# One decoder layer on one core: x transposed without its row factor, the factor applied after the products, fresh tiles for the first weights, and all low parts on VectorE

## The chip, the cores and the metric

The program runs on one core of a Trainium2 chip. The core has TensorE (PE, matmuls and transposes), VectorE (DVE), ScalarE (ACT), GpSimd (POOL) and SyncE (SP), which here only issues transfers. The metric is the device time of one execution in microseconds (us); lower is better.

## The reference, cut to what matters

One trunk layer on 256 tokens of width 1024:

```python
a = rms_norm(h, mix_norm_g[i])
z = a @ w_in[i]                       # 1024 x 3584, columns: q_a k_a v_a q_h f_h i_h g_h, 512 each
q = partial_rope(rms_norm(q, q_norm_g[i]), positions) * (ATTN_HEAD_DIM ** -0.5)
k = partial_rope(rms_norm(k, k_norm_g[i]), positions)
attn = dilated_attention(q, k, v).reshape(B, S, ATTN_WIDTH)
rec = hgrn2_mixer(q_h, f_h, i_h, g_h, lower_bounds[i], hgrn_norm_g[i])
h = h + jnp.concatenate([attn, rec], axis=-1) @ w_out[i]
m = rms_norm(h, ffn_norm_g[i])
h = h + moe_ffn(m, router_w[i], ...)  # 32 experts, top 4, every expert's 12 MB of f32 weights are read
h = h + (p[i] @ ple_proj[i]) * jax.nn.sigmoid(h @ ple_gate[i])
```

`rms_norm` multiplies each row (token) by one number, its row factor 1/sqrt(mean(x^2) + eps), and each column by g.

## The kernel before, in words

**Stages.** (1) The front: x is loaded and normalised, the seven z chunks of 512 columns are multiplied in the order ka, fh, qa, qh, va, ih, gh, and the attention and HGRN work on finished chunks is woven between the matmuls of the later chunks; then comes the product with w_out ("wo"). (2) Router and gates. (3) The 32 experts, each four gate-up tiles and two down tiles of 2 MB. (4) The last gate with `ple_gate` and the output.

**Products in two parts.** z and wo need more than one rounded pass: each f32 operand is split into a high part (rounded to fp32r) and a low part (the rest), and three matmuls are added: high x high, high x low, low x high. Weights are split in `split`: of every 1 MB tile ("place" 0 to 17: two per z chunk, four for wo) ScalarE writes two high parts (L249) and DVE or GpSimd subtracts two low parts (L250); the list `POOL_FIRST` names the places whose subtracts go to GpSimd, 10 of the 18. The parts live in a ring of 12 buffers (`highs`), three places' worth, so the split of place n waits until PE has used place n - 3.

**x.** `row_rstd` squares x (one half on ScalarE L307, one on DVE L308) and takes the power -0.5 on GpSimd (L302). A diagonal matrix `dg` of the row factors is built (L375), 16 matmuls x^T @ dg transpose and scale x (L380), and each of the eight 128-column blocks leaves PSUM times g as high part `ahi` (ScalarE L385) and low part `alo` (DVE L386).

**Order.** The order on each engine is set by a scheduler when the program is built. The list `STEPS` says after which half chunk which steps of the attention stream (q and k norms `qk_norm`, rotation, scores) and of the HGRN stream (`hgrn_f`, `hgrn_q`, the eight levels of `hgrn_levels`) come. The names used below: L653/L656/L302/L663/L664 are square, sum, power, scale by row, scale by g of a q or k norm; L675 to L680 the rotation, L687 the transposes behind it; L544, L546/L547, L556/L557, L583, L587 are one HGRN level (difference, two exponentials, two products, matmuls, masked copy).

**Memory.** Weights and large intermediates share a pool of 2 MB tiles (`Memory`), each of two halves; a 1 MB request takes a free half of a tile that is open, the first found. `fill` issues the next weight loads on SP's queue as tiles come free; the first 10 expert tiles are loaded while the front runs, and from then on each load waits for a tile to be used up.

Of the kernel before, what the change touches and what calls it, by code (L numbers as in the profile page):

```python
# [23 lines left out]
EPS = 1e-6  # L24
# [60 lines left out]
class Memory:  # L85
# [3 lines left out]
    def __init__(self):  # L89
        self.pools, self.room, self.tiles = [], [], []  # L90

# [4 lines left out]
    def open(self, kind):  # L96

        for k, n in enumerate(self.room):
            if n:
                self.room[k] -= 1  # L100
                g = dict(pool=k, kind=kind, busy=[0, 0], t=self.pools[k].tile([128, 4096], kind, name="g", tag="g"))
# [14 lines left out]

    def take(self, n, kind, shape):
        g = n == 1 and self.half(kind) or self.open(kind)
        assert g, ("full", n, kind)
        i = g["busy"].index(0) if n == 1 else 0  # L120
        g["busy"][i:i + n] = [1] * n
        a = g["t"][0:shape[0], 2048 * i:2048 * i + int(np.prod(shape[1:]))]
        if len(shape) > 2:
            names = "abc"[:len(shape) - 1]
            a = a.rearrange("p (%s) -> p %s" % (" ".join(names), " ".join(names)), **dict(zip(names[1:], shape[2:])))
        return a, (g, i, n)

# [9 lines left out]
def layer(ctx, tc, A, at):  # L137
# [60 lines left out]
    place = {k: i for i, k in enumerate(seq)}  # L198
    st = {"next": 0, "raw": 0, "cap": 0, "split": 0, "keep": 0}
    raw, parts, owner = {}, {}, {}  # L200
# [4 lines left out]
    def fill():  # L205
        while st["raw"] < st["cap"] and st["next"] < len(seq):
            k = seq[st["next"]]
            n = 2 if big(k) else 1
            keep = max([st["keep"]] + [a - len(held) for a in TILES[len(log):]])
            if not M.can(n) or M.left() - n < keep:  # L210
# [9 lines left out]
            else:  # L220
                shape = [128, 4, 512]
            t, i = M.take(n, F32, shape)
            if not place[k] or k == (("D", E - 1), 1):
# [59 lines left out]

    for tt in range(2):
        sp.dma_start(h[:, tt, :], A["x"][0, tt * 128:(tt + 1) * 128, :])
    ident = const("ident")
    rows = pers.tile([24, 128], F32, name="rows")
    sp.dma_start(rows[0:8], A["mix_norm_g"].rearrange("o (j p) -> (o j) p", p=128))
# [4 lines left out]
    gcol = pers.tile([128, 32], F32, name="gcol")  # L293

    power = pers.tile([128, 16], F32, name="power")
    pool.memset(power, -0.5)
# [32 lines left out]

    rstd = row_rstd("x")  # L330
    ahi = S.new([128, 8, T], F32R, "ahi")
# [32 lines left out]

    p0 = bank()
    pe.transpose(p0[:, :24], rows, ident[:24, :24])
    for k in range(2):
        pe.transpose(p0[:, 24 + 4 * k:28 + 4 * k], rows2[:, k:k + 255:2], ident[:4, :4])
    act.activation(gcol[:, 0:24], p0[:, :24], AF.Copy)
    act.activation(gcol[:, 24:32].rearrange("p (j k) -> p k j", k=2), p0[:, 24:32].rearrange("p (k j) -> p k j", k=2), AF.Copy)  # L370


    dg = carve(256).rearrange("p (a d) -> p a d", a=2)
    for tt in range(2):
        dve.tensor_scalar(dg[:, tt, :], ident, rstd[:, tt:tt + 1], None, op0=OP.mult)  # L375
    for j in range(0, 8, 2):
        b = bank()
        for jj in range(2):
            for tt in range(2):
                pe.matmul(b[:, jj * 256 + tt * 128:jj * 256 + tt * 128 + 128], h[:, tt, (j + jj) * 128:(j + jj) * 128 + 128],  # L380
                          dg[:, tt, :], start=True, stop=True)
        for jj in range(2):
            s = b[:, jj * 256:jj * 256 + 256]
            g = gcol[:, j + jj:j + jj + 1]
            act.activation(ahi[:, j + jj, :], s, AF.Copy, scale=g)  # L385
            dve.scalar_tensor_tensor(alo[:, j + jj, :], s, g, ahi[:, j + jj, :].bitcast(F32), op0=OP.mult, op1=OP.subtract)  # L386

# [101 lines left out]
    def hgrn_f(p):  # L489
# [4 lines left out]
        s, lf = B["W"]  # L494
        act.activation(s, p, AF.Sigmoid)
        yield
# [94 lines left out]
    def hgrn_gate(p):  # L591
        G2 = S.new([128, 2, 1024], F32, "G2")
        B.update(gt=G2[:, 0], oo=G2[:, 1])
        act.activation(B["gt"], p, AF.Tanh, scale=0.5)
        yield
# [5 lines left out]
    def hgrn_out():  # L601
# [48 lines left out]
    def qk_norm(p, gi, dst, scale):  # L650
# [125 lines left out]
    def evac(n):  # L776
        def f(p):
            act.activation(lazy(n), p, AF.Copy)
            yield
        return f  # L780
# [63 lines left out]
    def squares(n):  # L844
        for tt in range(2):
# [4 lines left out]
            else:  # L850
                act.activation(o, hs_, AF.Square, accum_out=ss4[:, n, tt:tt + 1])

    def busy(t, n, i):

        for k in range(n):
            with tc.issue_after(i):
                i = pe.matmul(t[:, 0:128], ones, ones, start=True, stop=True).ins

# [434 lines left out]
```

## Time and profile before

| | |
|---|---|
| median of 3 runs | 1148.01 us (1146.41 to 1151.06) |
| profiled execution | 1148.54 us, span 1146.8 us |
| PE busy | 1062.8 us (93% of the span) |
| DVE busy | 324.2 us (28%) |
| ACT busy | 204.8 us (18%) |
| POOL busy | 80.4 us (7%) |
| read from HBM | 430.51 MB, 376 GB/s over the span |

The span is the time from the first to the last event of the profiled execution, and the execution's own time is 1.7 us more. Busy shares are means over four stages with different limits, so the rows further down are cut by stage.

### The profile page before, as it was taken

How to read it: one execution, taken by the hardware profiler on the slowest of the kernel's cores; microseconds unless marked ns; L12 is line 12 of the kernel's file. 1: busy time of each engine (PE TensorE's matmuls, PEld its weight loads, DVE VectorE, ACT ScalarE, POOL GpSimd, SP SyncE). 2: the span in 40 equal slices, each digit the busy share in tenths (PEclk: the TensorE clock that was granted, in tenths of full speed). 3: DMA queues.
4: the chain of work that ended last, by engine and by line, in shares of the span. 5: the costliest groups of instructions: out<-in, count | busy, mean ns of one | idle time of the engine just before them, and what ended most of it. 6: DMA issues, size and time to landing. Idle time of an engine off the chain costs nothing. (4 is left out here: it accounts for less than half of the span.)

```text
span 1146.8 us, 12108 instructions
## 1 busy us (share of the span) xinstructions
PE 1062.8 (93%) x5045; PEld 467.3 (41%) x5045; DVE 324.2 (28%) x627; ACT 204.8 (18%) x395; POOL 80.4 (7%) x76
## 2 busy tenths in 40 slices
PE   6899899999999999999999999899999999999877
PEld 5787674333333333333333333333333333333235
DVE  5878733222121111211111111111211121111143
ACT  5646531011111111111111111111101111110030
POOL 4651140000000000000000000000000000000000
PEclk9999899999999999999999999999999999999998
DMA  8842568999999999999999999999989999999961
GB/s 287 288 149 87 203 264 366 427 428 426 427 429 427 428 428 428 427 428 427 427 427 429 428 428 426 414 426 427 427 348 419 427 424 428 429 427 427 429 253 37
DMA packets 44692, 432.41 MB, mean 377 GB/s; under 512 B 5980, under 2 KB 7672, under 8 KB 19928
## 3 DMA queue, kind: packets, MB, share of 16 engines
q1 hardware_dynamic: 44232, 430.66, 90.1%
q0 software_dynamic: 400, 0.92, 0.2%
q8 instruction: 42, 0.69, 0.2%
q14 instruction: 18, 0.15, 0.0%
HBM read 430.51 MB, written 1.05 MB: 376 GB/s over the span
## 5 line engine op out<-in xcount | busy, mean ns | idle before, releaser
L1108 PE MATMUL bk<-g,x 128*64 128x512 f32 x2048 | 468.8, 596 | 4.2 <-DMA g<-in_expert_w_gate_up 4.2
L1108 PEld LDWEIGHTS bk<-g,x 128*64 128x64 f32 x2048 | 144.9, 137 | 282.0 <-issue 263.5
L1142 PE MATMUL bk<-g,ht 128*64 128x512 f32 x1024 | 235.1, 596 | 16.3 <-DMA g<-in_expert_w_down 16.3
L1142 PEld LDWEIGHTS bk<-g,ht 128*64 128x64 f32 x1024 | 73.4, 137 | 154.2 <-issue 144.0
L1120 ACT ACTIVATE sgm<-gm 128x512 f32<-128x512 f32 x32 | 20.2, 630 | 377.4 <-DVE gm L1119 377.4
L1119 DVE TENSOR_SCALAR gm<-bk 128x512 f32<-128x512 f32 x32 | 22.1, 692 | 206.3 <-PE bk L1108 204.8
L925 PE MATMUL bk<-h,sx 128*64 128x512 f32 x256 | 67.0, 610 | 0.0
L1082 DVE TENSOR_SCALAR sg<-c_slot,posx,gates 128x128 f32<-128x128 f32 x64 | 19.3, 344 | 166.9 <-PE bk L1085 166.9
L917 POOL CAST sb<-c_sel 128x128 fp32r<-128x128 f32 x32 | 9.4, 296 | 810.2 <-PE bk L1098 802.8
L940 DVE TENSOR_TENSOR x<-bk,gcol 128x256 f32<-128x256 f32 x64 | 24.2, 420 | 131.8 <-PE bk L936 131.8
L1149 DVE SCALAR_TENSOR_TENSOR ylo<-bk,gs,yhi 128x512 fp32r<-128x512 f32 x32 | 24.0, 750 | 122.4 <-ACT yhi L1148 116.2
L250 POOL TENSOR_TENSOR lo<-g,hi 128x1024 fp32r<-128x1024 f32 x20 | 54.5, 2744 | 53.7 <-ACT hi L249 40.2
L1157 PE MATMUL pz<-yhi,so 64*128 64x512 f32 x128 | 29.3, 445 | 21.5 <-ACT yhi L1148 17.9
L1148 ACT ACTIVATE yhi<-bk,gs 128x512 fp32r<-128x512 f32 x32 | 22.0, 687 | 139.9 <-PE bk L1142 139.9
L249 ACT ACTIVATE hi<-g 128x1024 fp32r<-128x1024 f32 x36 | 37.4, 1056 | 19.8 <-issue 7.8
L1132 ACT ACTIVATE ht<-bk 128x512 f32<-128x512 f32 x32 | 19.1, 598 | 116.6 <-PE bk L1130 116.6
L927 ACT ACTIVATE xr<-bk 128x512 f32<-128x512 f32 x32 | 19.1, 597 | 112.1 <-PE bk L925 112.1
L914 DVE TENSOR_SCALAR sx<-c_slot,posx,rstd 128x64 f32<-128x64 f32 x64 | 17.2, 312 | 62.2 <-PE bk L925 62.2
L1157 PE MATMUL pz<-ylo,so 64*128 64x512 f32 x128 | 28.9, 440 | 5.4 <-DVE ylo L1149 5.4
L435 PE MATMUL pz<-hi,g 128*128 128x512 f32 x80 | 32.4, 405 | 1.6 <-DVE g L663 0.8
L437 PE MATMUL pz<-hi,g 128*128 128x512 f32 x80 | 32.2, 403 | 0.0
L436 PE MATMUL pz<-lo,g 128*128 128x512 f32 x80 | 31.9, 399 | 0.0
(254 smaller groups left out, 928.3 us busy)
## 6 DMA issues: line engine op xcount, KB each, us to landing
g<-in_expert_w_gate_up SPq DMA_DIRECT2D x128, 2048.0 KB, 31.9
g<-in_expert_w_down SPq DMA_DIRECT2D x63, 2048.0 KB, 36.1
g<-in_w_in SPq DMA_DIRECT2D x13, 1024.0 KB, 5.7
g<-in_w_out SPq DMA_DIRECT2D x4, 1024.0 KB
g<-in_ple_gate SPq DMA_DIRECT2D x4, 1024.0 KB, 18.6
g<-in_expert_w_down SPq DMA_DIRECT2D x2, 1024.0 KB, 35.5
h<-in_x SPq DMA_DIRECT2D x2, 512.0 KB, 4.3
g<-in_w_in SPq DMA_DIRECT2D x2, 512.0 KB, 4.4
```

The lines of the kernel that those rows point to most:

```text
L249: act.activation(hi, w[:, o:o + 2], AF.Copy)
L250: (pool if i in POOL_FIRST else dve).tensor_tensor(lo, w[:, o:o + 2], hi.bitcast(F32), OP.subtract)
L435: pe.matmul(o, ahi[:, j, s], hi[:, jj, :], start=j == 0, stop=False)
L436: pe.matmul(o, ahi[:, j, s], lo[:, jj, :], start=False, stop=False)
L437: pe.matmul(o, alo[:, j, s], hi[:, jj, :], start=False, stop=j == 7)
L925: i = pe.matmul(b[halves[n], :], s[:, tt, :], h[:, tt, n * 512:n * 512 + 512], start=tt == 0, stop=tt == 1, skip_group_check=True)
L940: xi = dve.tensor_tensor(x[:, :, n, :], b.rearrange("p (c n s) -> p c n s", c=4, n=2)[:, :, n, :], g, OP.mult)
L1108: pe.matmul(P[halves[n], :], x[:, j % 4, j // 4, :], w[:, j % 2, c:c + 512], start=e == 0 and j == 0, stop=j == 7 and e > 0, skip_group_ch ...
L1119: dve.tensor_scalar(gm, G, 7.0, None, op0=OP.min)
L1142: pe.matmul(P[halves[n], :], t[:, k, j, :], w[:, k, n * 512:n * 512 + 512], start=j == 0 and k == 0, stop=j == 1 and k == 3, skip_group_ch ...
L1149: dve.scalar_tensor_tensor(lo, P, g, hi.bitcast(F32), op0=OP.mult, op1=OP.subtract)
L1157: pe.matmul(acc[tt][n], t[halves[n], tt * 128:tt * 128 + 128], y[halves[n], :], start=e == 0 and y is R[e]["y"][0], stop=False, skip_group ...
```

## The change

Four edits. **(a)** x is transposed as it is (16 PE transposes, then times g as high and low part), without the row factor; nine matmuls on a tile of ones run before x is there, six more after the transposes. The factor is applied downstream: as a row of the broadcast tile `rB` where a chunk is feature-major (`hgrn_f`, `hgrn_q`: a DVE multiply of 128 x 1024 each from PSUM), as a scale of ScalarE's copy where it is token-major (v, i, gate), and through small factors `r2`, `rh`, `rstd` in the norms. The squares of x come after the eight blocks have left PSUM. **(b)** `POOL_FIRST` is empty: all 36 low parts are subtracted on DVE. **(c)** A 1 MB load opens an unused 2 MB tile while more than one is left, otherwise the half that has been free longest is taken; the reserve for intermediates (`TILES`) only holds back 2 MB loads. **(d)** The first splits are held behind certain blocks of x in the order of issue.

```diff
-POOL_FIRST = [1, 3, 4, 5, 8, 9, 12, 14, 16, 17, 18, 20, 23, 25, 28, 30]
+POOL_FIRST = []
+WARM = 9
+FRESH = 99
...
     def half(self, kind):
-        for g in self.tiles:
-            if g["kind"] == kind and 0 in g["busy"]:
-                return g
+        free = [(g["since"][i], k, g) for k, g in enumerate(self.tiles) if g["kind"] == kind for i in (0, 1) if not g["busy"][i]]
+        return min(free)[2] if free else None
...
+        g = self.half(kind) if n == 1 else None
+        if g and early and sum(self.room) > 1 and self.clock - min(g["since"][i] for i in (0, 1) if not g["busy"][i]) < early:
+            g = None
+        g = g or self.open(kind)
...
-            keep = max([st["keep"]] + [a - len(held) for a in TILES[len(log):]])
+            keep = max([st["keep"]] + [a - len(held) for a in TILES[len(log):]]) if big(k) else 0
...
-            act.activation(hi, w[:, o:o + 2], AF.Copy)
-            (pool if i in POOL_FIRST else dve).tensor_tensor(lo, w[:, o:o + 2], hi.bitcast(F32), OP.subtract)
+            with ExitStack() as late:
+                for x in st["order"][(1, 5, 7, 7)[2 * i + o // 2]] if i < 2 else ():
+                    late.enter_context(tc.issue_after(x))
+                act.activation(hi, w[:, o:o + 2], AF.Copy)
+                (pool if i in POOL_FIRST else dve).tensor_tensor(lo, w[:, o:o + 2], hi.bitcast(F32), OP.subtract)
...
-    rstd = row_rstd("x")
+    wz = pz()
+    busy(wz, WARM)
+    xb = [bank() for _ in range(4)]
+    for tt in range(2):
+        for j in range(8):
+            o = j % 2 * 256 + tt * 128
+            last = pe.transpose(xb[j // 2][:, o:o + 128], h[:, tt, j * 128:j * 128 + 128], ident)
...
+    busy(wz, 6, last.ins)
...
+    for j in range(8):
+        t = xb[j // 2][:, j % 2 * 256:j % 2 * 256 + 256]
+        g = gcol[:, j:j + 1]
+        i = act.activation(ahi[:, j, :], t, AF.Copy, scale=g)
+        d = dve.scalar_tensor_tensor(alo[:, j, :], t, g, ahi[:, j, :].bitcast(F32), op0=OP.mult, op1=OP.subtract)
+        st["order"].append((i.ins, d.ins))
+    with tc.issue_after(i.ins), tc.issue_after(d.ins):
+        rstd = row_rstd("x")
...
+    def factors():
+        for tt in range(2):
+            dve.tensor_scalar(dg[:, tt, :], ident, rstd[:, tt:tt + 1], None, op0=OP.mult)
+            pe.matmul(rr[:, tt * 128:tt * 128 + 128], ones, dg[:, tt, :], start=True, stop=True)
+        act.activation(rB, rr, AF.Copy)
...
-        act.activation(s, p, AF.Sigmoid)
+        dve.tensor_tensor(v4(s), v4(p), rB[:, None, :].to_broadcast([128, 4, 256]), OP.mult)
+        act.activation(s, s, AF.Sigmoid)
...
+        dve.tensor_tensor(v4(B["hq"]), v4(p), rB[:, None, :].to_broadcast([128, 4, 256]), OP.mult)
+        act.activation(sg, B["hq"], AF.Tanh, scale=0.5)
```

ScalarE at the start of the front, before (L307 is the square of x, L249 a high part of weights, L385 a block of x leaving PSUM):

```order
L307 ACTIVATE g,ssx<-h 128x1024
L369 ACTIVATE gcol<-bk 128x24
L370 ACTIVATE gcol<-bk 128x2x4
L480 ACTIVATE lbe<-lbe 128x8
L249 ACTIVATE hi<-g 128x1024 x2
L385 ACTIVATE g<-bk,gcol 128x256
L249 ACTIVATE hi<-g 128x1024
L385 ACTIVATE g<-bk,gcol 128x256 x2
L249 ACTIVATE hi<-g 128x1024
L385 ACTIVATE g<-bk,gcol 128x256 x3
```

The same place after the change (L319 the square, L259 the high parts, L402 the blocks of x):

```order
L361 ACTIVATE gcol<-pz 128x24
L362 ACTIVATE gcol<-pz 128x2x4
L402 ACTIVATE g<-bk,gcol 128x256 x4
L516 ACTIVATE lbe<-lbe 128x8
L402 ACTIVATE g<-bk,gcol 128x256
L259 ACTIVATE hi<-g 128x1024
L402 ACTIVATE g<-bk,gcol 128x256 x3
L319 ACTIVATE g,ssx<-h 128x1024
L259 ACTIVATE hi<-g 128x1024 x7
```

The blocks of x moved ahead of the square, and seven of the first eight high parts behind it.

DVE while PE works on the qa and qh chunks, before, up to the end of k's rotation (L680) and the sum for q's norm (L656):

```order
L502 TENSOR_SCALAR g<-g 128x1024
L504 SCALAR_TENSOR_TENSOR g<-g 128x1024
L250 TENSOR_TENSOR lo<-g,hi 128x1024
L679 TENSOR_TENSOR g<-g,cs 128x64 x2
L250 TENSOR_TENSOR lo<-g,hi 128x1024
L525 TENSOR_TENSOR ends<-g 128x4
L540 TENSOR_TENSOR g<-g 128x8x64
L680 TENSOR_TENSOR g<-g 128x8x8 x2
L556 TENSOR_TENSOR g<-g 128x8x64
L656 TENSOR_REDUCE s_562<-g 128x16
```

The same place after (L542 was L504, L260 a low part, L725/L726 the rotation, L699 the sum):

```order
L542 SCALAR_TENSOR_TENSOR g<-g 128x1024
L260 TENSOR_TENSOR lo<-g,hi 128x1024
L540 TENSOR_SCALAR g<-g 128x1024
L725 TENSOR_TENSOR g<-g,cs 128x64 x2
L260 TENSOR_TENSOR lo<-g,hi 128x1024
L565 TENSOR_TENSOR ends<-g 128x4
L580 TENSOR_TENSOR g<-g 128x8x64
L726 TENSOR_TENSOR g<-g 128x8x8 x2
L260 TENSOR_TENSOR lo<-g,hi 128x1024 x2
L699 TENSOR_REDUCE s_594<-g 128x16
```

Two more low parts, those of place 8, stand on DVE between the rotation of k and the sum for q.

DVE where PE finishes the last z chunk, before (L587 a masked copy, L544, L556, L557 of the next level):

```order
L587 COPY_PREDICATED g<-g,bk 128x512
L250 TENSOR_TENSOR lo<-g,hi 128x1024
L647 TENSOR_TENSOR g<-bk,g 128x256
L719 RECIPROCAL arden<-aden 128x4
L250 TENSOR_TENSOR lo<-g,hi 128x1024
L587 COPY_PREDICATED g<-g,bk 128x512
L544 TENSOR_TENSOR g<-g 128x1024
L587 COPY_PREDICATED g<-g,bk 128x512
L556 TENSOR_TENSOR g<-g 128x128x4
```

The same place after (L627 the masked copy, L584 and L596 the next level):

```order
L260 TENSOR_TENSOR lo<-g,hi 128x1024
L765 RECIPROCAL arden<-aden 128x4
L690 TENSOR_TENSOR g<-bk,g 128x256
L627 COPY_PREDICATED g<-g,bk 128x512
L260 TENSOR_TENSOR lo<-g,hi 128x1024 x2
L627 COPY_PREDICATED g<-g,bk 128x512
L584 TENSOR_TENSOR g<-g 128x1024
L627 COPY_PREDICATED g<-g,bk 128x512 x2
L584 TENSOR_TENSOR g<-g 128x1024
L596 TENSOR_TENSOR g<-g 128x128x4
```

The low parts of place 16, the 17th and 18th subtract on GpSimd before, now stand on DVE between two masked copies.

## Rows read from the trace of the kernel before

**Rows 1.** The page, part 4: the chain that ended last, by engine.

```profile
DMA 15%; PE 10%; ACT 1%; DVE 1%; issue 0%; DVEq 0%; ACTq 0%; SPq 0%
```

**Rows 2.** Windows: us, busy (instructions) by engine, granted clock, DMA share, GB/s.

```profile
37.82:67.33 29.51, 25.32 (x154) 22.97 (x154) 25.96 (x31) 17.92 (x22) 18.56 (x8) 0.94 0.58 196
67.33:115.40 48.07, 48.07 (x254) 38.50 (x253) 38.92 (x62) 29.87 (x58) 14.22 (x6) 1.00 0.38 124
115.40:144.22 28.82, 24.61 (x157) 19.92 (x156) 22.07 (x34) 14.56 (x46) 4.91 (x2) 0.88 0.55 205
...
180.36:1107.10 926.74, 871.88 (x3994) 309.29 (x3993) 180.91 (x380) 99.37 (x198) 10.55 (x33) 0.99 1.00 423
```

**Rows 3.** Timeline of SP's queue: start, length, engine, line, transfer, count.

```profile
166.30 0.81 SPq L228 DMA_DIRECT2D g<-in_expert_w_gate_up  x2
180.36 1.96 SPq L228 DMA_DIRECT2D g<-in_expert_w_down  x2
```

**Rows 4.** Timeline of PE, instructions after a wait: in brackets the wait and its releaser.

```profile
38.66 0.47 PE L435 MATMUL pz<-hi,g 128*128 128x512 f32 x1 [0.84 <-DVE g L663]
...
55.90 0.88 PE L687 MATMUL bk<-c_ident,g 128*128 128x128 f32 x4 [3.35 <-DVE g L680]
...
121.55 0.71 PE L583 MATMUL bk<-g 128*128 128x128 f32 x4 [2.11 <-DVE g L587]
...
124.24 0.63 PE L808 MATMUL pz<-hi,g 128*128 128x512 f32 x1 [1.53 <-ACT g L646]
```

**Rows 5.** Timelines of DVE and of GpSimd (POOL) in the front.

```profile
18.07 2.15 DVE L250 TENSOR_TENSOR lo<-g,hi 128x1024 fp32r<-128x1024 f32 x1 [0.41 <-ACT hi L249]
...
27.29 2.30 DVE L456 TENSOR_SCALAR n<-n 128x16 f32<-128x16 f32 x1
...
50.27 1.20 DVE L250 TENSOR_TENSOR lo<-g,hi 128x1024 fp32r<-128x1024 f32 x1
...
52.80 2.31 DVE L525 TENSOR_TENSOR ends<-g 128x4 f32<-128x4 f32 x1
...
118.03 2.83 DVE L557 TENSOR_TENSOR g<-g 128x512 f32<-128x512 f32 x1
...
27.14 2.41 POOL L250 TENSOR_TENSOR lo<-g,hi 128x1024 fp32r<-128x1024 f32 x1 [0.66 <-ACT hi L249]
...
115.19 5.13 POOL L250 TENSOR_TENSOR lo<-g,hi 128x1024 fp32r<-128x1024 f32 x2 [13.57 <-PE pz L436]
```

**Rows 6.** Timelines of PE, DVE and ACT at the start of the front.

```profile
15.98 0.39 PE L435 MATMUL pz<-hi,g 128*128 128x512 f32 x1
16.21 0.40 PE L436 MATMUL pz<-lo,g 128*128 128x512 f32 x1
...
17.14 0.50 PE L435 MATMUL pz<-hi,g 128*128 128x512 f32 x1 [0.31 <-ACT g L385]
...
5.94 1.22 DVE L308 SCALAR_TENSOR_TENSOR g<-h 128x1024 f32<-128x1024 f32 x1 [5.94 <-DMA h<-in_x]
...
6.97 0.19 ACT L369 ACTIVATE gcol<-bk 128x24 f32<-128x24 f32 x1 [1.19 <-PE bk L368]
...
12.10 0.47 ACT L385 ACTIVATE g<-bk,gcol 128x256 fp32r<-128x256 f32 x1 [1.41 <-PE bk L380]
...
15.89 1.20 ACT L385 ACTIVATE g<-bk,gcol 128x256 fp32r<-128x256 f32 x3
16.96 1.08 ACT L249 ACTIVATE hi<-g 128x1024 fp32r<-128x1024 f32 x1
```

**Rows 7.** Timelines of GpSimd and DVE: powers on GpSimd, and what DVE did meanwhile or after.

```profile
7.59 0.72 POOL L302 TENSOR_TENSOR rstdx<-vvx,power 128x2 f32<-128x2 f32 x1 [6.60 <-DVE vvx L311]
...
34.35 2.91 POOL L302 TENSOR_TENSOR r<-v,power 128x16 f32<-128x16 f32 x1 [1.86 <-DVE cs L466]
...
7.90 0.16 DVE L481 TENSOR_TENSOR lbm<-lbe 128x4 f32<-128x4 f32 x1 [0.28 <-ACT lbe L480]
...
37.29 1.23 DVE L663 TENSOR_TENSOR g<-pz,r 128x1024 f32<-128x1024 f32 x1 [2.94 <-POOL r L302]
```

More of the change, by code (lines that the diff above doesn't have):

```diff
@@ L89, in __init__ @@
     def __init__(self):
-        self.pools, self.room, self.tiles = [], [], []
+        self.pools, self.room, self.tiles, self.clock = [], [], [], 0
     def add(self, pool, n):
@@ L100, in open @@
                 self.room[k] -= 1
-                g = dict(pool=k, kind=kind, busy=[0, 0], t=self.pools[k].tile([128, 4096], kind, name="g", tag="g"))
+                g = dict(pool=k, kind=kind, busy=[0, 0], since=[0, 0], t=self.pools[k].tile([128, 4096], kind, name="g", tag="g"))
                 self.tiles.append(g)
@@ L115, in can, with take @@
         return any(self.room) or n == 1 and self.half(F32) is not None
-    def take(self, n, kind, shape):
-        g = n == 1 and self.half(kind) or self.open(kind)
+    def take(self, n, kind, shape, early=False):
+        g = self.half(kind) if n == 1 else None
+        if g and early and sum(self.room) > 1 and self.clock - min(g["since"][i] for i in (0, 1) if not g["busy"][i]) < early:
+            g = None
+        g = g or self.open(kind)
         assert g, ("full", n, kind)
-        i = g["busy"].index(0) if n == 1 else 0
+        i = min((g["since"][i], i) for i in (0, 1) if not g["busy"][i])[1] if n == 1 else 0
         g["busy"][i:i + n] = [1] * n
@@ L129, in give @@
         g, i, n = at
+        self.clock += 1
         g["busy"][i:i + n] = [0] * n
+        g["since"][i:i + n] = [self.clock] * n
         if not any(g["busy"]):
@@ L198, in layer @@
     place = {k: i for i, k in enumerate(seq)}
-    st = {"next": 0, "raw": 0, "cap": 0, "split": 0, "keep": 0}
+    st = {"next": 0, "raw": 0, "cap": 0, "split": 0, "keep": 0, "order": []}
     raw, parts, owner = {}, {}, {}
@@ L282, in const @@
         return t
-    for tt in range(2):
-        sp.dma_start(h[:, tt, :], A["x"][0, tt * 128:(tt + 1) * 128, :])
+    sp.dma_start(h[:, 0, :], A["x"][0, 0:128, :])
     ident = const("ident")
+    sp.dma_start(h[:, 1, :], A["x"][0, 128:256, :])
     rows = pers.tile([24, 128], F32, name="rows")
@@ L293, in layer @@
     gcol = pers.tile([128, 32], F32, name="gcol")
+    ones = pers.tile([128, 128], F32, name="ones")
+    dve.memset(ones, 1.0)
     power = pers.tile([128, 16], F32, name="power")
@@ L328, in pz, with busy @@
         return ps.tile([128, 1024], F32, name="pz", bufs=2)
-    rstd = row_rstd("x")
+    def busy(t, n, i=None):
+        for k in range(n):
+            with tc.issue_after(i) if i is not None else nullcontext():
+                i = pe.matmul(t[:, 0:128], ones, ones, start=True, stop=True).ins
+    wz = pz()
[5 more added lines that the diff above has]
+            last = pe.transpose(xb[j // 2][:, o:o + 128], h[:, tt, j * 128:j * 128 + 128], ident)
+    w = pz()
+    p0, rr = w[:, 0:32], w[:, 512:768]
+    pe.transpose(p0[:, :24], rows, ident[:24, :24])
+    for k in range(2):
+        last = pe.transpose(p0[:, 24 + 4 * k:28 + 4 * k], rows2[:, k:k + 255:2], ident[:4, :4])
+    act.activation(gcol[:, 0:24], p0[:, :24], AF.Copy)
+    act.activation(gcol[:, 24:32].rearrange("p (j k) -> p k j", k=2), p0[:, 24:32].rearrange("p (k j) -> p k j", k=2), AF.Copy)
+    busy(wz, 6, last.ins)
     ahi = S.new([128, 8, T], F32R, "ahi")
@@ L363, in layer @@
     sel2 = const("sel")
[L365 to L386, printed above, removed]
+    for j in range(8):
[6 more added lines that the diff above has]
+        rstd = row_rstd("x")
+    rB = carve(256)
+    dg = rB.rearrange("p (a d) -> p a d", a=2)
+    r2 = pers.tile([128, 2], F32, name="r2")
+    rh = pers.tile([128, 2], F32, name="rh")
+    def factors():
[3 more added lines that the diff above has]
+        act.activation(rB, rr, AF.Copy)
+        dve.tensor_tensor(r2, rstd, rstd, OP.mult)
+        dve.tensor_scalar(r2, r2, 1.0 / 64, None, op0=OP.mult)
+        dve.tensor_scalar(rh, rstd, 0.5, None, op0=OP.mult)
+    factors()
     streams = [deque(), deque()]
@@ L593, in hgrn_gate @@
         B.update(gt=G2[:, 0], oo=G2[:, 1])
-        act.activation(B["gt"], p, AF.Tanh, scale=0.5)
+        for tt in range(2):
+            c = slice(tt * 512, tt * 512 + 512)
+            act.activation(B["gt"][:, c], p[:, c], AF.Tanh, scale=rh[:, tt:tt + 1])
         yield
@@ L777, in f @@
         def f(p):
-            act.activation(lazy(n), p, AF.Copy)
+            for tt in range(2):
+                c = slice(tt * 512, tt * 512 + 512)
+                act.activation(lazy(n)[:, c], p[:, c], AF.Copy, scale=rstd[:, tt:tt + 1])
             yield
@@ L851, in squares @@
                 act.activation(o, hs_, AF.Square, accum_out=ss4[:, n, tt:tt + 1])
[L853 to L857, printed above, removed]
     def logits(n):
```

15 lines of the change are left out of this document (9 added, 6 removed).

## The prediction

> **What bounds the kernel now.** I read the chain that ended last first, then windows by stage, then the queue of the weight loads, then the waits inside the front.
>
> The chain's largest share is DMA, 15% against 10% for PE [rows 1]. The windows say why: from 180.36 to 1107.10 us the DMA engines are busy all the time, at 423 GB/s [rows 2], so this stage lasts as long as its bytes do. Its start is what can move: the queue issues the last two of the ten tiles loaded ahead at 180.36, when the router has let their space go, and the pair before at 166.30, when the wo product is over [rows 3]. From there on nothing in the order of the loads is changed. So what the front saves reaches the end one for one, and only the front counts.
>
> The front, from 13.76 to 166.3, is a stretch in which PE is nearly always at work: 48.07 of 48.07 us between 67.33 and 115.40. It falls short in two windows, 25.32 of 29.51 and 24.61 of 28.82, and there the granted clock is 0.94 and 0.88 too [rows 2]. The waits in them are four: 0.84 us for DVE's L663 (it must empty a PSUM tile), 3.35 for DVE's L680 (the rotation of k), 2.11 for DVE's L587 (a masked copy of an HGRN level), 1.53 for ScalarE's L646 [rows 4]. They sum to 7.83 us. Three end on DVE itself; the fourth I put down to the same late attention and level steps, which is a choice. PE is in order, so a late DVE step is its loss; the waits of the others are not.
>
> **Why DVE is late.** Its instructions are stretched while a subtract of GpSimd runs. The same 128 x 1024 subtract takes 1.20 us at 50.27 and 2.15 at 18.07; L456, on 16 columns, takes 2.30 at 27.29, under a GpSimd subtract of 2.41 that began at 27.14; L525, on four, takes 2.31 at 52.80; L557 takes 2.83 at 118.03, inside GpSimd's pair from 115.19 [rows 5]. Undisturbed, a DVE operation on four columns takes 0.16, as L481 does [rows 7]. I count 17 such DVE instructions between the first at 18.07 and the last at 118.03, and their excess over equal instructions is about 28 us. The last two sit straight ahead of two of PE's waits: L525 holds up L680, L557 the copy for which PE waits at 121.55.
>
> A rule of the Trainium skill says the same (SBUF — State Buffer, "Who interferes with whom"): a DVE instruction with two SBUF inputs contends with a GpSimd instruction that reads SBUF, and the loser is blocked for the whole instruction. The rows agree for the subtracts.
>
> **The change, part by part.**
>
> *(b) All subtracts on DVE.* Added to DVE: 20 x 1.20 = 24 us, all in the front. Taken away: the 28 us of excess. So DVE's total hardly falls. What changes is where the time lies. The excess fell on whatever stood next; the subtracts stand where the order puts them, and part of that is idle now: DVE waits 2.94 us for the power on GpSimd before L663 at 37.29 [rows 7], and after the change two subtracts stand in that gap.
>
> *(a) The factor downstream.* Added to DVE: two multiplies from PSUM of 1.23 us each, like L663 [rows 7], and about a dozen small operations of L481's kind, 0.16 each; together some 4 us. On PE two small f32 matmuls with the ones tile, which no row shows: I take 0.5 us, between nothing and two of 0.40, what a matmul of 512 columns takes [rows 6]. ScalarE's copies cut in two add less than 1 us, and it is not waited for there.
>
> At the start the gain looks large and is not. Before, x^T could not be made until the squares, the power and `dg` were done; ScalarE had the column g at 6.97 + 0.19 and its first block of x only at 12.10 [rows 6], some 5 us later. After, blocks follow at once. But PE needs split weights too, and ScalarE has the same list in either order. After: g at about 7.9 (DVE had x's second half at 5.94, a transfer that now follows the identity's; the transposes behind it I put at 1.5); five blocks at 0.40 and a small exponential to 10.1; a high part at 1.08 to 11.1; three blocks to 12.3; the square, as long as a high part, to 13.4; the next high part to 14.5 [rows 6]. DVE subtracts the first low part by 12.3, then come three blocks, its own square (1.22) and the second low part, done by 16.1. PE can do 7 matmuls before that and then runs through: with 0.23 us each (15.98 to 16.21) its 24th ends at 16.1 + 17 x 0.23 = 20.1. Before, nine were done at 17.14 and it ran through from there [rows 6]: the 24th at 17.14 + 15 x 0.23 = 20.6. So the start brings 0.5 us and the extra matmuls take it back: 0. Bounds: 4.2 us of gain, if PE finds work for all of the time by which ScalarE starts earlier (12.1 - 7.9), and 1.5 of loss, if PE has fallen to the lower of its two clock levels (1.2 of 2.4 GHz) in the gaps before 16.1 and gets half the matmuls done for some 3 us.
>
> *k's norm (0.84 and 3.35).* After: ka's 48 matmuls end near 20.1 + 24 x 0.23 + 0.5 = 26.1. ScalarE ends place 4's second high part and the square, a pass each of 1.08, by 28.2; DVE sums by 29.6, the power takes 2.91 and small steps around it bring r to 33.0; the two subtracts of place 5 fill the time to 34.7; L709 ends at 36.1. PE's fh chunk (96 matmuls of half the columns, so half of 0.23 each) ends at 37.4. No wait: -0.84. Then L710, the multiply of fh, four subtracts (4.8), the first half of the rotation (1.2), the scan and smaller steps: 16 to 17 us of DVE work behind 36.1 with one short wait for the logarithm, so the last rotation step lies near 52. PE wants it after the 48 matmuls of qa and 28 of qh, 11.2 + 3.3 us behind 37.4, at 51.9. I leave 0.3: 3.35 becomes 0.3.
>
> *After the last z chunk (2.11 and 1.53).* The pair of subtracts ahead of two masked copies waits for PE's last z matmuls, as GpSimd's pair at 115.19 did for 13.57 us [rows 5], and holds the copies; L556 and L557 behind them are no longer stretched. Following the order from there with these durations PE meets one wait of DVE again, 1.9 us, for the copy after the two level products. 3.64 becomes 1.9.
>
> *The clock.* In the two windows the grant was 0.94 and 0.88. Its cost lies between nothing (all of it inside the gaps) and 0.06 x 25.3 + 0.12 x 24.6 = 4.5 us. I take the middle, 2.2, as given back with the gaps.
>
> *(c) and (d).* Fresh tiles start some loads of the front earlier; PE waits for no weight there in any row, so nothing. They cost something only if the expert tiles find no room; the ten ahead still have until 180.36 and the queue's pauses to land in.
>
> **Sum.** -0.5 + 0.5 at the start, -0.84, -3.35 + 0.3, -3.64 + 1.9, -2.2: -7.8 us. The profiled execution took 1148.54 (span 1146.8 and 1.7 around it): 1140.7. It lies 0.5 above the median of 1148.01, so on the median 1140.
>
> **The rivals.** Half a per cent, 5.7 us, is about what a measurement of this kernel tells from no change.
>
> *R1, DVE waits for the powers.* GpSimd's two powers of 2.91 us [rows 7] may stretch DVE as its subtracts did. Then the two subtracts in the gap of k's power move behind it, L709 ends at 38.4 in place of 36.1, and the same happens at q's: 2.3 + 2.1 us back, 1144.6. The rule of the Trainium skill quoted above would have it so, since the power reads SBUF too. Against it: L481, with two SBUF inputs, ran 0.16 us in the middle of the power at 7.59 [rows 7], but that is four columns of work.
>
> *R2, the waits only move.* DVE carries 28 us more and 28 less; if its in-order queue loses at new places what it wins at the old, for instance behind the constants (the row of norm weights lands later, since a sixth weight tile is now queued ahead of it), PE's waits stay near 8 us: 1146 to 1149.
>
> *R3, slower.* Each moved pair may stand ahead of level work while it waits for PE to release a `highs` buffer; GpSimd took such waits at no cost (13.57 at 115.19). With ten pairs and 1.4 us each DVE is 14 us later, PE's filler cannot cover it, and the front ends 6 us later than before: 1154. The point is 0.8 us a pair; above it the forecast's gain is gone.
>
> *R4, the gain doesn't arrive.* If the ten tiles ahead were to land after the router is done, the stream would start late by as much: 1148. They had some 4 us to spare: two tiles of 2 MB from 166.30 take about 10 us at the stream's 423 GB/s [rows 2, 3]. All of it moves with the front, so I give it little.
>
> **Chances.** Forecast 0.62, R1 0.12, R2 0.13, R3 0.09, R4 0.04. The forecast's own range: -7.8 with the clock's other half and 3.7 of the start's bound, 1134, to 1144. Over 0.5% faster: nearly all of the forecast and a quarter of R1, 0.62; over 0.5% slower: R3 and a little of R2, 0.10; between: 0.28. The range that holds 8 in 10 goes from 1134 to 1148: it leaves out R3 and little else.
>
> **What would show it.** Right: no DVE instruction of the front stretched; the pair of D tiles issued 7 to 9 us before 180.36; the first z matmul near 11 but the 24th not before 20; no wait of over 1 us ahead of k's transposes; windows at a clock of 1.00. Wrong: subtracts on DVE that follow the powers without overlap (R1); PE waits for DVE copies of 2 us and more after the z chunks, with a subtract waiting for PE just ahead (R3); the pair issued early and the last weight landing no earlier (R4).

## The result, and the profile after

The median of 5 runs is 1137.43 us (1136.54 to 1138.43) against 1148.01 (by now also of 5 runs): a ratio of 0.9906, 95% interval 0.9893 to 0.992. The profiled execution took 1138.26, its span is 1136.5. Forecast was 1140.

The chain that ended last, by engine, of the changed kernel (of before: [rows 1]): DMA went from 15% to 12%, PE from 10% to 13%.

```profile
PE 13%; DMA 12%; DVE 1%; ACT 1%; issue 0%; DVEq 0%; ACTq 0%
```

Windows of the changed kernel by stage: from the end of the fh chunk through k's and q's part of the front, the part where PE is always busy, the part behind the z chunks, the router, the experts, the last stage (us, busy and instructions by engine, granted clock, DMA share, GB/s):

```profile
38.19:61.90 23.71, 23.25 (x149) 21.09 (x150) 22.66 (x38) 17.35 (x22) 3.86 (x2) 1.00 0.88 315
61.90:114.45 52.55, 52.55 (x285) 41.87 (x284) 43.52 (x73) 34.97 (x65) 0.00 (x0) 1.00 0.23 81
114.45:136.00 21.55, 20.13 (x136) 16.50 (x136) 15.72 (x32) 12.98 (x46) 0.00 (x0) 1.00 0.49 180
156.74:174.25 17.51, 16.40 (x107) 14.66 (x106) 8.72 (x40) 3.88 (x8) 1.24 (x3) 0.81 0.61 240
174.25:1101.48 927.23, 872.38 (x3994) 309.08 (x3994) 180.96 (x381) 99.39 (x198) 10.46 (x33) 0.99 1.00 423
1101.48:1136.50 35.02, 25.61 (x112) 19.39 (x112) 19.04 (x31) 12.16 (x20) 0.00 (x0) 0.96 0.10 35
```

The router and the last stage of the kernel before, cut at the same instructions:

```profile
166.11:180.36 14.25, 13.14 (x107) 11.40 (x106) 8.72 (x40) 3.88 (x8) 1.24 (x3) 1.00 0.75 295
1107.25:1146.80 39.55, 29.39 (x112) 22.64 (x112) 19.04 (x31) 12.15 (x20) 0.00 (x0) 0.85 0.09 31
```

Three things are to be seen. The two windows of the front with a clock of 0.94 and 0.88 [rows 2] are at 1.00 now. The router, with the same 107 instructions, takes 3.26 us longer, at a clock of 0.81 where it had 1.00. The last stage, which the change does not touch, takes 4.53 us less, at 0.96 where it had 0.85.

The queue of the loads, the last two pairs loaded ahead [rows 3]: 9.4 us earlier at the end of wo, but only 6.1 earlier when the router is done.

```profile
156.94 0.80 SPq L235 DMA_DIRECT2D g<-in_expert_w_gate_up  x2
174.25 1.95 SPq L235 DMA_DIRECT2D g<-in_expert_w_down  x2
```

PE's waits at the places of [rows 4], in brackets the wait and its releaser (L709 was L663, L733 was L687, L623 was L583):

```profile
38.65 0.47 PE L471 MATMUL pz<-hi,g 128*128 128x512 f32 x1 [0.46 <-DVE g L709]
...
53.31 1.03 PE L733 MATMUL bk<-c_ident,g 128*128 128x128 f32 x8
...
118.82 2.05 PE L623 MATMUL bk<-g 128*128 128x128 f32 x16 [1.42 <-DVE g L627]
```

0.84 became 0.46; 3.35 is gone; 2.11, 1.53 and a further one of 0.57 behind them became one of 1.42.

So the 10.3 us by which the spans differ are: 9.37 won up to the first transposes of the router (166.11 to 156.74), 3.26 lost in the router, 0.34 lost among the experts (926.89 became 927.23), 4.53 won in the last stage.

### The profile page after: what moved, and what is told of

It is laid out like the page before. It is cut to its first block, busy times and chain, and to the rows that moved or that the text cites. A ratio compares the mean times of both kernels' runs of the same rounds, so it can differ in the third digit from the quotient of the medians.

```text
span 1136.5 us, 12153 instructions
## 1 busy us (share of the span) xinstructions
PE 1062.7 (94%) x5063; PEld 466.8 (41%) x5063; DVE 322.4 (28%) x658; ACT 207.1 (18%) x399; POOL 27.7 (2%) x55
## 3 DMA queue, kind: packets, MB, share of 16 engines
HBM read 430.51 MB, written 1.05 MB: 380 GB/s over the span
## 5 line engine op out<-in xcount | busy, mean ns | idle before, releaser
L1197 PE MATMUL pz<-yhi,so 64*128 64x512 f32 x128 | 30.1, 454 | 20.9 <-ACT yhi L1188 17.5
L260 DVE TENSOR_TENSOR lo<-g,hi 128x1024 fp32r<-128x1024 f32 x36 | 43.1, 1221 | 4.8 <-ACT hi L259 4.7
L259 ACT ACTIVATE hi<-g 128x1024 fp32r<-128x1024 f32 x36 | 37.0, 1061 | 19.4 <-PE pz L472 9.7
L1197 PEld LDWEIGHTS pz<-yhi,so 64*128 64x128 f32 x128 | 12.6, 188 | 44.9 <-ACT yhi L1188 35.3
```

The costliest lines, as they stand in the source:

```text
L1197: pe.matmul(acc[tt][n], t[halves[n], tt * 128:tt * 128 + 128], y[halves[n], :], start=e == 0 and y is R[e]["y"][0], stop=False, skip_group ...
```

## The experiments

Twelve kernels, four to a chip (e1 to e4, e5 to e8, e9 to e12). Ratios are to the kernel before on the same chip; its medians there were 1148.88, 1148.05 and 1147.70 us, so a difference of 1 us between medians of two chips shows nothing by itself, and the two columns on the right have to bear it out. "D pair" is when the last two tiles ahead are issued, "last stage" the time from the first transposes of h there to the end of the span, both in the profiled execution.

| run | median us | ratio, 95% interval | D pair | last stage |
|---|---|---|---|---|
| before | 1148.01 | | 180.36 | 39.55 |
| changed | 1137.43 | 0.9906 (0.9893 to 0.992) | 174.25 | 35.02 |
| e1 (b) alone | 1139.38 | 0.9917 (0.99 to 0.9935) | 170.11 | 39.7 |
| e2 changed without (b) | 1143.66 | 0.9951 (0.9939 to 0.9964) | 178.85 | 34.8 |
| e3 changed without (c) | 1138.3 | 0.9899 (0.9881 to 0.9916) | 175.31 | 33.8 |
| e4 (b) and (c) | 1138.1 | 0.9901 (0.9887 to 0.9916) | 169.68 | 39.8 |
| e5 e4, other last stage | 1134.19 | 0.9878 (0.9857 to 0.9899) | 169.83 | 35.1 |
| e6 changed, old last stage | 1140.69 | 0.9929 (0.9908 to 0.9951) | 174.25 | 38.6 |
| e7 changed, router filled | 1133.61 | 0.9871 (0.985 to 0.9893) | 172.02 | 32.8 |
| e8 before, other last stage | 1143.57 | 0.9951 (0.9931 to 0.997) | 180.31 | 34.8 |
| e9 e4, GpSimd reads | 1162.22 | 1.0127 (1.0111 to 1.0142) | 193.04 | 39.0 |
| e10 e4, GpSimd writes | 1140.69 | 0.9949 (0.9936 to 0.9963) | 172.18 | 39.3 |
| e11 e4, five splits first | 1131.72 | 0.986 (0.9845 to 0.9876) | 170.17 | 33.0 |
| e12 e7, last stage as changed | 1135.95 | 0.9898 (0.9882 to 0.9913) | 172.57 | 35.0 |

**Which edit pays (e1 to e4).** In e1 one line of the kernel before is changed:

```diff
-POOL_FIRST = [1, 3, 4, 5, 8, 9, 12, 14, 16, 17, 18, 20, 23, 25, 28, 30]
+POOL_FIRST = []
```

> The kernel before with edit (b) alone: all 36 low parts on DVE. Theory (DVE stretched by GpSimd's subtracts is what PE waited for): 1138 to 1142 us, no stretched DVE instruction between 18 and 120 us, the waits of 3.35 and 2.11 us gone or below 1.5, the granted clock of the front at 1.00, and most of the 10 us won. Rival 1 (the gain is that of x transposed raw and its earlier start): 1146 to 1149, waits of 3 us and more still there. Rival 3 (DVE held behind the moved subtracts): above 1150.

It won nine tenths of the change alone. Two short DVE instructions are still longer than their equals, and both stand beside GpSimd work that is no subtract of weights: L455 (0.47 in place of 0.17, at 25.84, beside the router weights' multiply L796) and L658 (1.02, at 55.07, beside a memset). PE's waits for DVE in the front are one of 1.12 and two under 0.4, the clock is 1.00 up to the D pair, and that is issued 10.25 us earlier; 1.8 us of it were gone again at the end. The one wait of over 1 us, and the clock of the whole front:

```profile
117.45 2.30 PE L583 MATMUL bk<-g 128*128 128x128 f32 x16 [1.12 <-DVE g L587]
```

```profile
0.00:170.11 170.11, 158.03 (x941) 132.67 (x942) 120.59 (x238) 94.19 (x177) 15.60 (x23) 1.00 0.64 230
```

e2 puts the old list back into the changed kernel:

```diff
-POOL_FIRST = []
+POOL_FIRST = [1, 3, 4, 5, 8, 9, 12, 14, 16, 17, 18, 20, 23, 25, 28, 30]
```

> The changed kernel with edit (b) undone: GpSimd subtracts the ten places of before again. Theory: DVE instructions are stretched again, PE's waits at k's rotation and behind the z chunks come back, with two multiplies of 1.2 us more on DVE: 1147 to 1151 us. Rival 1 (raw x): 1137 to 1141.

The stretched instructions came back as expected, but not the wait at k's rotation: PE waits at other places, for L709 (2.43 and 0.77 us), for the factors of x (1.00) and behind the z chunks (0.67, 1.28, 0.38 and 0.35). Nor did the time come back: 1143.66, a miss of 3.3 us below the range. In its DVE timeline the ends (four columns) take 2.37 us and the two small products with the identity 4.77 together; the longest wait is PE's for L709:

```profile
20.21 4.77 DVE L415 TENSOR_SCALAR g<-c_ident,rstdx 128x128 f32<-128x128 f32 x2 [0.61 <-POOL rstdx L314]
...
56.63 2.37 DVE L565 TENSOR_TENSOR ends<-g 128x4 f32<-128x4 f32 x1
```

```profile
43.43 0.47 PE L471 MATMUL pz<-hi,g 128*128 128x512 f32 x1 [2.43 <-DVE g L709]
```

Its D pair is issued only 1.5 us before that of the kernel before, so 4 us must have been won behind it. They are in the table: a last stage of 34.8 us, as in the changed kernel. That made the last stage the next question. Against the changed kernel its front is 7.9 us longer (the router begins at 164.60 in place of 156.74), and its router 3.3 shorter: the clock does not fall there.

e3 takes (c) back in the changed kernel:

```diff
-        free = [(g["since"][i], k, g) for k, g in enumerate(self.tiles) if g["kind"] == kind for i in (0, 1) if not g["busy"][i]]
-        return min(free)[2] if free else None
+        for g in self.tiles:
+            if g["kind"] == kind and 0 in g["busy"]:
+                return g
...
-            t, i = M.take(n, F32, shape, FRESH)
+            t, i = M.take(n, F32, shape)
```

> The changed kernel with edit (c) undone: the first loads share tiles as before. Theory: 1136 to 1140 us, since PE waits for no weight in the front with either rule. Rival 2 (the earlier loads are part of the gain): 1141 and more, with a PE or ScalarE wait for a load of w_in or w_out in the first 60 us.

e4 brings (b) and (c) into the kernel before, without (a) and (d):

```diff
+POOL_FIRST = []
+FRESH = 99
...
+            t, i = M.take(n, F32, shape, FRESH)
```

> Edits (b) and (c) in the kernel before, without (a) and (d): x is still scaled while it is transposed. Theory: like (b) alone, 1138 to 1142 us, within 2 us of the changed kernel, so (a) and (d) bring nothing or under 2 us. Rival 1: 1146 to 1149. In all four kernels of this call the place where the granted clock falls (router, last stage, or nowhere) is looked up; if it falls at different places in kernels whose last stage is the same program, the 4.5 us that the last stage won is no part of the change.

Both came out at the changed kernel's time, 1138.3 and 1138.1. (c) is worth 0.9 us (e3 against the changed kernel) or 1.3 (e4 against e1), which these intervals do not tell from nothing. e3 does not isolate it: ScalarE waits 3.27 us for a load of w_in at 35.59, the sign that rival 2 had named, the router begins 1.05 us later, and the last stage has an order of its own (five splits first) and is 1.2 shorter. (a) and (d) together bring 0.7, but the columns show that this is a balance: without them the D pair is issued 4.6 us earlier (1.3 of it in the front, 3.3 in the router, whose clock does not fall in e4) and the last stage takes 4.8 longer.

**The last stage (e5, e6, e8, e11).** There ScalarE and DVE split the gate's weights (L1231 and L1232, eight instructions on each) and empty four blocks of h (L1221). ScalarE in the kernel before, and PE's wait for it:

```profile
1109.28 7.68 ACT L1231 ACTIVATE g<-g 128x1024 fp32r<-128x1024 f32 x8
1116.86 1.55 ACT L1221 ACTIVATE g<-bk 128x512 fp32r<-128x512 f32 x3
...
1117.49 0.61 PE L1251 MATMUL pz<-g 128*128 128x512 f32 x1 [2.17 <-ACT g L1221]
```

And in the changed kernel, with L1271 for L1231 and L1261 for L1221:

```profile
1103.16 5.79 ACT L1271 ACTIVATE g<-g 128x1024 fp32r<-128x1024 f32 x6
1108.85 0.58 ACT L1261 ACTIVATE g<-bk 128x512 fp32r<-128x512 f32 x1
1109.32 2.00 ACT L1271 ACTIVATE g<-g 128x1024 fp32r<-128x1024 f32 x2
...
1109.48 0.50 PE L1291 MATMUL pz<-g 128*128 128x512 f32 x1 [0.26 <-ACT g L1261]
```

The second block now stands behind six splits and not behind eight. No edit asks for that: the scheduler that sets the order came to it by way of the changes ahead. e5 and e8 force this order on e4 and on the kernel before:

```diff
+                for x in blk[2] if (n, hf) == GATE[3] else ():
+                    late.enter_context(tc.issue_after(x))
                 act.activation(hi[:, o:o + 2], w[:, o:o + 2], AF.Copy)
```

e11 sets five in place of six in e4, and e6 gives the changed kernel the old order, with the block of j = 2 behind all splits (`spl`):

```diff
-                for x in blk[2] if (n, hf) == GATE[3] else ():
+                for x in blk[2] if (n, hf) == GATE[3] or (n, hf) == GATE[2] and o else ():
...
+                for x in spl[-1:] if j == 2 else ():
+                    for y in x:
+                        late.enter_context(tc.issue_after(y))
                 act.activation(o, b, AF.Copy)
```

> Edits (b) and (c) without (a) and (d), and in the last stage the order that the changed kernel has there: ScalarE and DVE empty the second block of h behind six of the eight splits of the gate, not behind all eight. Theory (this order is what shortened the last stage by 4.5 us, and it came along with (a) by way of the scheduler): 1132 to 1135 us, 4 to 5 below the 1138.1 without it, the stage from the transposes of h to the end near 35 us in place of 39.7. Rival (the last stage was shorter by chance, or because of what the front does to the clock): 1137 to 1139.

> The kernel before with only the last stage's order changed to that of the changed kernel, as in the first run of this call. Theory: 1143 to 1145 us, 4 to 5 us faster than before with a front that is untouched (the D pair still issued at 180). Rival (chance): 1147 to 1149.

> The changed kernel with the last stage's order of before: all eight splits, then the second block of h. Theory: 1141 to 1143 us, PE's wait of 2.1 us for ScalarE there again, and a granted clock under 1 behind it. Rival (chance): 1137 to 1139.

> Edits (b) and (c), and in the last stage the second block of h behind five of the eight splits of the gate, as the kernel with the filled router happened to have it. Theory (the order there is worth another 2 us): 1131.5 to 1133 against 1134.2 with six and 1138.1 with eight. Rival: 1134 to 1135.

e5 gains 3.9 us over e4 (its last stage is 4.7 shorter), e8 gains 4.4 over the kernel before (0.9951, measured on the same chip) with its front as it was, and e11 another 2.5 over e5 (last stage 2.1 shorter): as the theory had them. In e11, as in e7, the last copies of ScalarE stand in another order too, so the 2.5 belong to the whole order of that stage and not to the number of splits alone. e6 loses 3.3, at 0.3 below the range for it; PE's wait is there again:

```profile
1111.23 0.50 PE L1298 MATMUL pz<-g 128*128 128x512 f32 x1 [2.17 <-ACT g L1267]
```

So the last stage's 4 us come from the order, and that order came with (a) and (d): e1 and e4, without them, have the old one. Chance is refuted.

**The router (e7, e12).** The 24 products with the router's weights take 2.76 us before and 4.78 after, behind the same wait of 1.11:

```profile
168.25 1.08 PE L876 MATMUL bk<-rw,g 128*128 128x32 f32 x8 [1.11 <-DVE g L870]
...
170.07 2.76 PE L876 MATMUL bk<-rw,g 128*128 128x32 f32 x24
```

```profile
158.88 1.08 PE L916 MATMUL bk<-rw,g 128*128 128x32 f32 x8 [1.11 <-DVE g L910]
...
160.71 4.78 PE L916 MATMUL bk<-rw,g 128*128 128x32 f32 x24
```

e7 puts eight small matmuls into that wait; e12 does so too, and holds the last stage's order by lines like those above, since in e7 it had moved to five splits:

```diff
         if not n:
             bl = bank()
+            busy(wz, 8, last.ins)
```

> The changed kernel with eight small matmuls on the tile of ones in the router, where PE waits 1.11 us for DVE's copy of the first transposes. Theory (the fall of the granted clock to 0.51 in the router follows that gap): no fall there, the pair of D tiles issued 3 us earlier, 1134 to 1135 us. Rival (the fall has to do with what ran long before, not with the gap): the clock falls in the router all the same, 1137 to 1138; or it falls elsewhere, in the last stage, and the time stays.

> The changed kernel with the router's gap filled, as in the earlier run, but the last stage's order held to that of the changed kernel (six splits, block, two splits), which the earlier run had not kept. Theory: 1134.5 to 1136, so that of the 3.8 us about 2 are the router's clock and 2 the last stage. Rival 1 (all of it was the router): 1133 to 1134. Rival 2 (all of it was the last stage): 1137 to 1138.

The fall is gone from the router in both, and the router takes 14.7 us in place of 17.5. The D pair comes only 2.2 and 1.7 us earlier, not 3: the clock fell at the start in both, for some 6 us from 13 or 14 on, and the router begins 0.6 and 1.1 us later. From 16 to 20 us, the changed kernel and then e12:

```profile
16.00:20.00 4.00, 3.63 (x16) 2.94 (x17) 4.00 (x9) 3.38 (x4) 1.54 (x1) 1.00 1.05 388
```

```profile
16.00:20.00 4.00, 3.69 (x9) 2.95 (x10) 4.00 (x9) 2.34 (x3) 1.55 (x1) 0.50 1.05 387
```

By the medians, of e7's 3.8 us (0.4 more than expected) 2.3 are the last stage's order, and 1.5 are the router's gain less the loss at the start. The 1.5 are not clear of noise: e12's ratio and the changed kernel's, 0.9898 and 0.9906, have intervals that overlap. The wait is not the whole cause of the fall: the kernel before and e1, e2, e4, e5 and e8 to e11 have one of 1.10 or 1.11 at the same instruction and no fall there; the changed kernel, e3 and e6 have it. Nor is it shown that the filling took the fall away: in e2 the wait is not filled and the router's clock stays at 1.00, and e2 too had the low clock at the start (0.50 from 16 to 20).

**Contention by itself (e9, e10).** e4 with work on GpSimd that nothing else in the program uses, at the ten places of the old list:

```diff
+            for a in range(8) if i in OLD else ():
+                c = slice(a % 4 * 128, a % 4 * 128 + 128)
+                pool.tensor_tensor(scr, w[:, o + a // 4, c], hi[:, a // 4, c].bitcast(F32), OP.subtract)
```

and in e10 in its place

```diff
+            if i in OLD:
+                pool.tensor_tensor(scr[:, 0:4], w[:, o, 0:4], hi[:, 0, 0:4].bitcast(F32), OP.subtract)
+                for a in range(8):
+                    pool.memset(scr, 0.0)
```

> Edits (b) and (c) without (a) and (d), all low parts on DVE, and beside that extra work on GpSimd which nobody waits for: at the ten places of before it subtracts the same operands once more, in eight pieces of 128 columns, into a scratch tile. Theory (DVE is stretched by GpSimd instructions that read SBUF): DVE instructions under these pieces are stretched, one to two us each time where they have two SBUF inputs, PE's waits for DVE come back, 1144 us or more, against 1138.1 without the extra work. Rival (the gain came from where the subtracts stand and from DVE's shorter duration, not from contention): no DVE instruction stretched, 1137 to 1140.

> The same with extra work that only writes: at each place one subtract of four columns and eight memsets of 128 columns on the scratch tile. Theory (it is the reading that blocks): no DVE instruction stretched by the memsets, 1137 to 1140. Rival (any GpSimd instruction blocks DVE): stretched as in the run with reads, 1142 and more.

DVE and GpSimd in e9:

```profile
30.87 1.21 DVE L667 TENSOR_REDUCE s<-g 128x16 f32<-128x1024 f32 x1
...
44.13 1.22 DVE L674 TENSOR_TENSOR g<-pz,r 128x1024 f32<-128x1024 f32 x1 [7.58 <-POOL r L313]
...
47.89 1.47 DVE L258 TENSOR_TENSOR lo<-g,hi 128x1024 fp32r<-128x1024 f32 x1
...
53.59 0.95 DVE L513 TENSOR_SCALAR g<-g 128x1024 f32<-128x1024 f32 x1
...
13.81 25.38 POOL L261 TENSOR_TENSOR scr<-g,hi 128x128 f32<-128x128 f32 x30 [5.33 <-ACT hi L257]
...
41.19 2.90 POOL L313 TENSOR_TENSOR r<-v,power 128x16 f32<-128x16 f32 x1
```

Some DVE instructions are stretched, but by 0.27 us each (0.68 to 0.95, 1.20 to 1.47), not by one to two; that the pieces are short may be why, which no run shows. The time went another way, which neither theory had: k's power stood on GpSimd behind the pieces and started at 41.19, so DVE waited 7.58 us and PE behind it 7.47, and for the same step of q's norm 6.20 (at 78.10). The 1162 us therefore says nothing of the stretching. e10 does:

```profile
28.86 2.09 POOL L262 MEMSET scr<- 128x128 f32 x8
...
28.91 1.23 DVE L258 TENSOR_TENSOR lo<-g,hi 128x1024 fp32r<-128x1024 f32 x1 [0.18 <-ACT hi L257]
...
50.96 3.66 POOL L260 TENSOR_TENSOR scr<-g,hi 128x4 f32<-128x4 f32 x1 [7.44 <-issue]
```

Under memsets the subtract takes its 1.23 us. The time, 1140.69, lies 0.7 above the range: the powers again queue behind the extra work (PE waits 1.52 for L675 at 63.45).

## Why the prediction was right, and where it was not

- **DVE is late because GpSimd stretches it: right.** With the ten pairs on DVE the stretching is gone: 36 subtracts at 1.22, and one small step left (L491, 0.59 in place of 0.17, beside GpSimd's L842). e1 shows that the list alone brings the gain, e2 that the stretching returns with it, and e9 and e10 that, for DVE instructions with two SBUF inputs, GpSimd's reading does it and its writing does not. One of the 17 that the prediction counted, L658 at 59.92, stood beside a memset and not a subtract. That GpSimd's queue held back the powers is no rival: the power of k's norm began after 1.86 us in which GpSimd waited for DVE [rows 7], that of q's at 61.01, when DVE's L658 was over (60.93). What the stretching alone costs in time was not measured: in e9 another wait covers it.

The group of the subtracts on the changed kernel's page (count, busy us, mean ns, idle time ahead and its main releaser):

```profile
L260 DVE TENSOR_TENSOR lo<-g,hi 128x1024 fp32r<-128x1024 f32 x36 | 43.1, 1221 | 4.8 <-ACT hi L259 4.7
```

- **R1, the powers hold DVE: refuted.** Beside q's power of 2.90 us DVE does two subtracts, at 1.18 each:

```profile
56.24 2.90 POOL L314 TENSOR_TENSOR r<-v,power 128x16 f32<-128x16 f32 x1 [2.26 <-DVE v L703]
...
57.03 2.36 DVE L260 TENSOR_TENSOR lo<-g,hi 128x1024 fp32r<-128x1024 f32 x2 [0.94 <-ACT hi L259]
```

- **"L709 ends at 36.1": wrong by 2.4.** It ended at 38.50, where it had ended before, and at the time that R1 gave (38.4), but not for R1's reason: the first subtract began 1.1 us before the power was over. The forecast had the sum done at 29.6. It ended at 32.53, behind small steps that waited 3.98 us for a row of norm weights (before: 1.15, until 25.37), the late constants that R2 named; so the power ran to 35.90. The step also took the two subtracts of place 5 to be ready when the power began. ScalarE makes their high parts only at 33.72, behind a cosine that waits 3.74 us for the same small steps; the subtracts start at 34.80 and L709 stands behind them. So 0.84 became 0.46 and not 0, an error of 0.46.

```profile
27.78 0.23 DVE L386 TENSOR_SCALAR g<-g 128x128 f32<-128x128 f32 x1 [3.98 <-DMA g<-in_hgrn_norm_g]
...
31.32 1.21 DVE L699 TENSOR_REDUCE s<-g 128x16 f32<-128x1024 f32 x1
...
33.00 2.90 POOL L314 TENSOR_TENSOR r<-v,power 128x16 f32<-128x16 f32 x1 [2.84 <-DVE ang L495]
...
33.50 0.22 ACT L499 ACTIVATE cs<-ang 128x16 f32<-128x16 f32 x1 [3.74 <-DVE ang L497]
...
33.72 1.99 ACT L259 ACTIVATE hi<-g 128x1024 fp32r<-128x1024 f32 x2
...
34.80 2.36 DVE L260 TENSOR_TENSOR lo<-g,hi 128x1024 fp32r<-128x1024 f32 x2 [0.56 <-ACT hi L259]
...
37.28 1.22 DVE L709 TENSOR_TENSOR g<-pz,r 128x1024 f32<-128x1024 f32 x1
```

- **The start: right in this execution, with luck.** The 24th z matmul starts at 20.22, where 20.1 was forecast for its end; fh ends at 38.19 against 37.82 before, a loss of 0.37 for a forecast of 0. The loss that the prediction gave as a bound, a fallen clock ahead of 16.1, came in e2, e7 and e12: with the same two waits just before (1.75 or 1.76 us, then 0.76 or 0.77) their 24th starts at 21.50 to 22.04. The changed kernel and e6 have these waits and no fall. What decides it is open.
- **k's rotation: right.** 3.35 became 0 (forecast 0.3); DVE ends it at 51.81 (forecast near 52), PE comes for it at 53.31.
- **After the z chunks: right, a little better.** 3.64 became 1.42 (forecast 1.9), and the wait of 0.57 behind them is gone too. Ahead of its 36 subtracts DVE waited 4.8 us, 4.7 of them for ScalarE: none of them waited for a buffer from PE itself, and R3 is out. R2 is out too but for its late constants: the waits fell to 1.88 in all.
- **The clock: perhaps under-sized, and sought in the front alone.** Up to the router 9.37 us were won, 7.8 forecast. The waits and the start make 6.15 of it (0.38 + 3.35 + 2.79 - 0.37); 3.2 are left, where 2.2 were put for the clock. The clock can account for all of it: from the end of fh to the router PE has 657 instructions before and 656 after, its busy time fell by 3.21 us, and the granted clock rose from 0.96 to 1.00. But e4, at 1.00 too and with 658, is busy for 114.73 us, so busy time does not go by the clock alone, and the clock's share is not shown. Then the router gave 3.26 back, which no term and no rival had.

From the end of fh to the router, before and after:

```profile
37.82:166.11 128.29, 119.53 (x657) 98.59 (x657) 92.27 (x140) 68.28 (x139) 48.17 (x25) 0.96 0.51 180
```

```profile
38.19:156.74 118.55, 116.32 (x656) 95.67 (x657) 89.24 (x157) 70.50 (x142) 9.64 (x11) 1.00 0.52 192
```

- **"Only the front counts": the step that failed.** It rested on the order of the loads, which is indeed unchanged: the stream ran 0.34 us longer than before. But the order of ScalarE and DVE in the last stage did change, and 4.53 us of the 10.3 come from there. It stood in the order of the changed program, which the prediction compared in the front only, since the edits end there. That the total came out near 1140 is in part luck: this gain and the router's loss nearly cancel, with 1.3 us left over.

By edits: (b) is worth 9.5 us alone (e1 against the kernel before on its chip) and 6.2 in the changed kernel (e2; 4.7 between the profiled executions). (a) and (d) cost 2.6 (e6 against e4, the old order of the last stage in both, but on two chips) and bring another order there, worth 3.3 to 4.4 (e6, e5, e8). The kernel that keeps (b) and (c), leaves (a) and (d) out and sets the last stage's order, e11, takes 1131.72 us: 5.7 less than the changed kernel.

## What to carry to other kernels

Where an in-order engine is late, look first for its instructions that take longer than their equals, and at what runs beside them on another engine; here 24 us of work moved onto the busier engine made it earlier. Compare the whole program's order before and after, not only near the edit: a scheduler may answer a change in the first stage with another order in the last. A gain read off one stage is safe only with the stages behind it, at their clock.

## What the runs showed of the hardware that was not expected

- GpSimd can lose too, over several instructions: its subtract of four columns took 3.66 us in e10, where others took 0.20, while DVE worked through five instructions, two of them subtracts on 1024 columns; it ended as DVE began its sum. Its power lost as well there: begun at 32.98, while a DVE subtract ran from 32.71 to 33.94, it took 3.72 us in place of 2.90.
- DVE instructions with one input are stretched as well: `TENSOR_SCALAR` on 1024 columns from 0.68 to 0.95 in e9, and on two times 128 columns to 4.77 in e2. The sum (L667, 1.21 us in e9) is not. The Trainium skill (SBUF — State Buffer, "Who interferes with whom") says that `tensor_scalar` can contend and a reduction never does, and that a GpSimd instruction that only writes does not disturb a DVE instruction with two SBUF inputs; these rows and e10 agree. A DVE instruction with one input is another case: L658 on 16 columns took 1.01 us beside a memset in the kernel before (and 1.02 in e1), against 0.17 for the same step of k's norm at 34.10.

```profile
59.92 1.01 DVE L658 TENSOR_SCALAR v<-s 128x16 f32<-128x16 f32 x1
...
59.95 0.95 POOL L518 MEMSET g<- 128x1024 f32 x1 [1.74 <-DVE s L656]
```

- The power on GpSimd reads SBUF for 2.90 us and does not stretch DVE. By the same rule of the Trainium skill it should (SBUF — State Buffer, "Who interferes with whom": a GpSimd instruction that reads SBUF contends with a DVE instruction that has two SBUF inputs); the trace does not agree.
- The granted clock fell in the router in three kernels and not in nine others with the same wait there. What decides it stays open: it was gone in both runs that filled the wait, but in both the clock had fallen near the start, and e2, where it fell at the start and the wait was not filled, shows no fall in the router either.
